# Two pools for the experts' first rooms, pinned first loads, and pools at multiples of 1 KB

## The chip, the core and the metric

The kernel runs on one core of a Trainium2 chip. The core has five engines with queues of their own: TensorE (PE in the profile; its weight loads are PEld), VectorE (DVE), ScalarE (ACT), GpSimd (POOL) and SyncE (SP). SP computes nothing here; it issues the loads of the weights to 16 DMA engines. The data lie in a memory of 128 partitions, in which the program places tiles from pools.

The metric is the device time of one execution in microseconds (us), as the median of several runs.

## The reference

Two blocks follow each other on 256 tokens of width 1024, all in float32. The first is a hybrid layer (attention and a gated delta rule). The second has a mixer with two groups of heads and then a layer of experts:

```python
def second_block(x, p, positions, w_in, ...):
    ...
    mixed = jnp.concatenate([rmsnorm_2(o_m, g_out_mla[i]), rmsnorm_2(o_s, g_out_sb[i])], axis=-1)
    h = h + mixed @ w_o[i]
    h = h + moe(rmsnorm_2(h, g_moe[i]), w_router[i], b_router[i], w_gu[i], b_gu[i], w_dn[i], b_dn[i])
    u = rmsnorm_2(h, g_ple[i])
    h = h + jax.nn.sigmoid(u @ w_ple_gate[i]) * (p[i] @ w_ple_proj[i])

def moe(u, w_router, b_router, w_gu, b_gu, w_dn, b_dn):
    """Top-4-of-32 clamped-SwiGLU experts on u (B, S, D)."""
    logits = jnp.dot(xt, w_router) + b_router
    top_logit, top_e = lax.top_k(logits, TOP_K)
    ...
        hh = jnp.dot(xs, w_gu[e]) + b_gu[e]
        glu, lin = jnp.split(hh, 2, axis=-1)
        act = glu * jax.nn.sigmoid(SWIGLU_ALPHA * glu) * (lin + 1.0)
        return jnp.dot(act, w_dn[e]) + b_dn[e]
```

There are 32 experts. `w_gu` of one is 1024 x 2048 and `w_dn` is 1024 x 1024, 12 MB together, and each is read once: 384 loads of 1 MB (1,048,576 bytes).

## The kernel before

**Stages.** The first block and the mixers of the second run up to about 557 us. There `w_in`, `w_uq`, `w_ukv` and `w_o` come in through three rooms `raw` of the pool `st` (8 KB of each partition, one load each), are split into a high and a low part (`piece`, `split`: ACT copies, DVE subtracts, lines 315 and 316), and PE multiplies. Then the router chooses, and the experts run from about 582 us on. In that stage the weights are not split: PE multiplies straight from the rooms that the loads fill (line 1370).

**The experts.** `units` puts the experts in pairs, but for one that stands alone with twice the rows and one single at the end. A pair takes 16 loads of `w_gu` (eight steps of one load for each of the two experts) and 8 of `w_dn`. `pieces` yields the loads in the order in which PE uses them, and `run` consumes them in that order.

**The rooms.** `load` takes its rooms in a fixed turn from the list `raws`. For the experts the list is: four rooms `raw` of the pool `raw2`, three rooms `raw` of `st`, two `whi` and two `wlo` of `raw2`, two `whi` and two `wlo` of `st`. These are 15 rooms of 8 KB. `ahead` (line 1148) asks for the first 11 loads and `refill` (line 1489) for all others. In SP's queue 15 loads stand ahead of the first one that has to wait for an expert's product, that of a room whose content PE has used. A room is loaded again once PE has used what is in it.

**What lies under the rooms.** The pool `raw2` is opened where the pools of the mixers have been closed. Those are `wa` (eight tiles `w4` of 4 KB, 32 KB in all: the name `soon` in the code) and above it `wb` (76 KB: the name `w`). `soon` has the latent vectors, the tokens' queries and keys, and in the end the scores of the second half of the latent attention, `mla(1)`: its last readers are the transposes in `softmax_T` (line 385; the helper's line 304 in the profile). `wb` has all else, up to the turning of the last heads' output (`out_T`, line 1030, and the split at its end). `raw2` has eight rooms, 64 KB: the first four lie over `wa`, the others over the foot of `wb`. The framework lets the first load into a pool wait until all that lay under that pool has been read.

**What sets the order.** Each engine runs its own queue in order, and a wait at its head holds back what stands behind it. A scheduler of the framework sorts the instructions within the queues, except those that the code pins with `tc.keep_in_program_order` (the products and transposes of the experts' stage). The loads are not pinned. SP's queue also holds every load to at most eight in flight, by eight semaphores in turn (`DMAHW0` to `DMAHW7`).

```python
    raw2 = ctx.enter_context(tc.tile_pool(name="raw2", bufs=1))

    raws[:] = [(raw2, "raw", RAW2), (st, "raw", RAW), (raw2, "whi", 2), (raw2, "wlo", 2), (st, "whi", HL), (st, "wlo", HL)]
    parts.append((raw2, 2))
    ...
            ready = ahead(order, RAW + RAW2 + 4)
```

Of the kernel before, what the change touches and what calls it, by code (L numbers as in the profile page):

```python
# [7 lines left out]
F32 = mybir.dt.float32  # L8
# [7 lines left out]
P = 128  # L16
# [51 lines left out]
def tile_net(ctx: ExitStack, tc: tile.TileContext, a: dict, dbg=None):  # L68
    nc = tc.nc
    V, A, G, T, SY = nc.vector, nc.scalar, nc.gpsimd, nc.tensor, nc.sync  # L70
    dbg = dbg or {}

    cst = ctx.enter_context(tc.tile_pool(name="cst", bufs=1))
    st = ctx.enter_context(tc.tile_pool(name="st", bufs=1))
    sm = ctx.enter_context(tc.tile_pool(name="sm", bufs=4))
# [17 lines left out]
    wr = cst.tile([P, 8, 32], F32, name="wr")  # L93
    bguT = cst.tile([P, 32, 16], F32, name="bguT")

    RAW, HL = 3, 2
    raws = [(st, "raw", RAW)]
    parts = [(st, HL)]
    count = [0, 0]

    def slots():
        return sum(n_ for _, _, n_ in raws)

    def load(src, kc, n, pool=None, rows="(k p) n -> p k n"):

        if pool is None:
            i = count[0] % slots()
            count[0] += 1
            for pool, name, nb in raws:
                if i < nb:  # L110
                    break
                i -= nb
        else:
            (pool, nb), name = pool, "raw"
        raw = pool.tile([P, 2048], F32, name=name, bufs=nb)
        SY.dma_start(raw[:, :kc * n].rearrange("p (k n) -> p k n", k=kc), src.rearrange(rows, p=P))
        return raw

    def piece(src, kc, n, raw=None, by=None):

        if raw is None:
            raw = load(src, kc, n)
        i = count[1] % sum(n_ for _, n_ in parts)
        count[1] += 1
        pool, nb = parts[0] if i < parts[0][1] else parts[1]
        hi = pool.tile([P, 2048], F32R, name="whi", bufs=nb)
        lo = pool.tile([P, 2048], F32R, name="wlo", bufs=nb)
        m = kc * n
        split(hi[:, :m], lo[:, :m], raw[:, :m], by)
        v = lambda t: t[:, :m].rearrange("p (k n) -> p k n", k=kc)  # L130
        return v(hi), v(lo)

    def rows_piece(W, i, pool=None):
        nh, k0 = i // 2, (i % 2) * 4
        return load(W[k0 * P:(k0 + 4) * P, nh * 512:(nh + 1) * 512], 4, 512, pool)
# [255 lines left out]
    def rope(wk, dst, src, cos2, sin2, nh):  # L391
# [5 lines left out]
        V.tensor_tensor(t2[:, :, 16:32], src[:, :, 0:16], bm(sin2[:, 16:32], nh), ALU.mult)  # L397
        V.tensor_tensor(dst, t1, t2, ALU.add)

    keep = Pool(ctx.enter_context(tc.tile_pool(name="keep", bufs=1)), w4=4)  # L400

    ORDER = "01kstvo"
# [2 lines left out]
    pp = cp.enter_context(tc.tile_pool(name="pp", bufs=4, space=bass.MemoryType.PSUM))  # L405
    with ExitStack() as c1:
        both = ctx.enter_context(tc.tile_pool(name="both", bufs=1))
        pm = c1.enter_context(tc.tile_pool(name="ps", bufs=4, space=bass.MemoryType.PSUM))
        c2 = c1.enter_context(ExitStack())
        wk = c2.enter_context(tc.tile_pool(name="wk", bufs=1))  # L410
# [12 lines left out]
        for i in (2, 1):  # L423
            SY.dma_start(ctab[i], a["const"][:, cuts[i]:cuts[i + 1]])
        uinc, ustr, lstr, ones = (cc(k) for k in ("uinc", "ustr", "lstr", "ones"))
        first = [load(w_in[k0 * P:(k0 + 4) * P, 4096:4608], 4, 512) for k0 in (0, 4)]
        rows = [("conv_w", 96), ("gdn_norm_w", 1), ("g_cq_2", 3), ("g_ckv_2", 2),
                ("g_out_mla_2", 4), ("g_out_sb_2", 4), ("g_attn_2", 8), ("g_ple_2", 8)]
        vr = wk.tile([P, P], F32, name="vrow1")
        at = 0  # L430
        for n, k in rows:
            voff[n] = 16 + at
            src = a[n]
            src = src.rearrange("o t (c p) -> (o t c) p", p=P) if n == "conv_w" else src.rearrange("o (c p) -> (o c) p", p=P)
# [679 lines left out]
    RAW2 = 4  # L1114

    raw2 = ctx.enter_context(tc.tile_pool(name="raw2", bufs=1))

    raws[:] = [(raw2, "raw", RAW2), (st, "raw", RAW), (raw2, "whi", 2), (raw2, "wlo", 2), (st, "whi", HL), (st, "wlo", HL)]
    parts.append((raw2, 2))
    NE = 32  # L1120
    NJ = 15
    wgu = a["w_gu_2"].rearrange("o e d f -> (o e d) f")
# [4 lines left out]
    def pieces(units):  # L1127


        for i in range(len(units) + 1):  # L1130
            if i < len(units):
                rs = [p["row"]() for p in units[i]["places"]]
                for k in range(8):
                    for r in rs:
                        yield wgu[bass.ds(r + k * P, P)], 1, 2 * D, "(k p) n -> p k n"
            if i:
                rs = [p["row"]() for p in units[i - 1]["places"]]
                for q in range(4):
                    for r in rs:
                        yield wdn[bass.ds(r + q * 2 * P, 2 * P)], 2, D, "(p k) n -> p k n"  # L1140
            if i == EMB:
                yield a["w_ple_proj_2"][0], 2, D, "(k p) n -> p k n"
# [4 lines left out]

    def ahead(order, n, pool=None):

        return [(load(src, kc, m, pool, rows), kc, m) for src, kc, m, rows in (next(order) for _ in range(n))]  # L1150

    def in_register(ap):

# [8 lines left out]
    with ExitStack() as c3:  # L1162
# [43 lines left out]
        with ExitStack() as c4:  # L1206
# [6 lines left out]
            for i in range(1, NE):  # L1213
                if len(units[-1]["places"]) == 1 and DBL not in (i, i - 1):
                    units[-1]["places"].append(places[i])
                else:
                    units.append(unit([places[i]], i))
            order = pieces(units)
            ready = ahead(order, RAW + RAW2 + 4)
            rr, ut = [], []  # L1220

# [262 lines left out]
        def run(units, order, ready, more=None, room=None):  # L1484
# [11 lines left out]
            def nxt():  # L1496
                if not ready:
                    ready.extend(ahead(order, 1))
                raw, kc, m = ready.pop(0)
                return raw[:, :kc * m].rearrange("p (k n) -> p k n", k=kc)  # L1500
# [279 lines left out]
```

## Time and profile before

| | |
|---|---|
| Time, median of 3 runs | 1570.43 us (1569.9 to 1571.59) |
| The profiled execution | 1570.8 us, its span 1568.9 us |
| PE busy | 1431.5 us, 91% of the span |
| DVE, ACT, POOL busy | 39%, 27%, 2% |
| Read from memory | 483.48 MB |

The span is the time from the first to the last recorded instruction; 1.9 us of the profiled execution's time lie around it. Busy shares are averages over stages that have different limits, so the view that matters is the one that cuts the span into stretches. A matmul's row shows its whole way through the array, and matmuls overlap, so a PE that is busy all the time can still have room. In a timeline a row starts with its start and its length in us; `x4` merges four instructions, and the bracket at the end says how long the engine was idle ahead of it and what ended that.

### The profile page before, as it was taken

To read this page: it belongs to the slowest core of one execution; us is meant where nothing else is said; L and a number is where in the kernel's file an instruction comes from. 1 tells how busy PE (TensorE), PEld (TensorE's weight loads), DVE (VectorE), ACT (ScalarE), POOL (GpSimd) and SP (SyncE) were. 2 spreads that over 40 slices of the span, in tenths; PEclk is the share of its full clock that TensorE was granted. 3 is DMA by queue.
4 is the path that set the end of the run, shared out by engine and by line. 5 is a ranking of instruction groups with operands and counts; after the bars stand their busy time and mean duration, and the time that the engine had idled before them with its cause. 6 is when DMAs were issued, how large, how long until landed. Compare 5 with 4: busy or idle time off the path is not lost. (4 is left out here: it accounts for less than half of the span.)

```text
span 1568.9 us, 20018 instructions
## 1 busy us (share of the span) xinstructions
PE 1431.5 (91%) x7922; PEld 883.2 (56%) x7922; DVE 619.3 (39%) x1215; ACT 418.6 (27%) x638; POOL 27.1 (2%) x39
## 2 busy tenths in 40 slices
PE   6999998999889989989888998999988889989887
PEld 6889898999689864424334334434433324424335
DVE  6868865456656662112123122112312202302236
ACT  5543644443447621101001001101100101101124
POOL 0000100000000000000000000000000000000000
PEclk9999999999899989999999999999999999999998
DMA  7544244355344189999999999999999999999981
GB/s 241 163 150 150 90 141 130 108 188 173 127 132 141 55 345 421 421 421 421 421 421 419 421 421 421 421 421 420 421 421 421 421 420 420 421 422 421 421 350 67
DMA packets 108541, 487.58 MB, mean 311 GB/s; under 512 B 14766, under 2 KB 23356, under 8 KB 59292
## 3 DMA queue, kind: packets, MB, share of 16 engines
q1 hardware_dynamic: 108300, 485.87, 78.2%
q8 instruction: 64, 1.05, 0.3%
q0 software_dynamic: 144, 0.39, 0.1%
q14 instruction: 33, 0.27, 0.0%
HBM read 483.48 MB, written 2.75 MB: 310 GB/s over the span
## 5 line engine op out<-in xcount | busy, mean ns | idle before, releaser
L1370 PE MATMUL ph<-raw,xs 128*64 128x512 f32 (+1 forms) x936 | 241.7, 594 | 5.7 <-DMA raw<-in_w_gu_dram 5.6
L1370 PE MATMUL ph<-wlo,xs 128*64 128x512 f32 (+1 forms) x552 | 192.3, 594 | 4.8 <-DMA wlo<-in_w_gu_dram 4.8
L1370 PE MATMUL ph<-whi,xs 128*64 128x512 f32 (+1 forms) x560 | 194.6, 594 | 2.0 <-DMA whi<-in_w_gu_dram 2.0
L316 DVE TENSOR_TENSOR wlo<-raw,whi 128x2048 fp32r<-128x2048 f32 (+4 forms) x73 | 158.0, 2165 | 91.8 <-ACT whi L315 91.7
L212 PE MATMUL pm<-w,wlo 128*128 128x256 f32 x640 | 182.5, 286 | 6.6 <-DVE wlo L316 6.6
L210 PE MATMUL pm<-w,whi 128*128 128x256 f32 x640 | 185.1, 290 | 3.3 <-ACT whi L315 3.3
L1557 DVE COPY hs<-ph 128x512 f32<-128x512 f32 x34 | 23.5, 692 | 406.4 <-PE ph L1370 406.4
L211 PE MATMUL pm<-w,whi 128*128 128x256 f32 x640 | 183.0, 286 | 0.0
L315 ACT CAST whi<-raw 128x2048 fp32r<-128x2048 f32 (+4 forms) x73 | 131.9, 1806 | 141.3 <-PE pm L211 88.1
L1370 PE MATMUL pm<-raw,act 128*64 128x512 f32 (+1 forms) x520 | 137.9, 597 | 29.0 <-DMA raw<-in_w_dn_dram 29.0
L1370 PEld LDWEIGHTS ph<-raw,xs 128*64 128x64 f32 (+1 forms) x936 | 78.1, 138 | 144.9 <-issue 130.8
L1557 ACT COPY hs<-ph 128x512 f32<-128x512 f32 x34 | 19.9, 586 | 412.6 <-PE ph L1370 412.6
L212 PEld LDWEIGHTS pm<-w,wlo 128*128 128x128 f32 x640 | 124.0, 194 | 7.5 <-DVE wlo L316 7.5
L210 PEld LDWEIGHTS pm<-w,whi 128*128 128x128 f32 x640 | 124.3, 194 | 4.1 <-ACT whi L315 3.9
L211 PEld LDWEIGHTS pm<-w,whi 128*128 128x128 f32 x640 | 124.5, 194 | 0.3
L1460 DVE SCALAR_TENSOR_TENSOR yl<-pm,gs,yh 128x512 fp32r<-128x512 f32 x32 | 24.0, 750 | 251.1 <-ACT yh L1459 250.4
L1370 PEld LDWEIGHTS ph<-wlo,xs 128*64 128x64 f32 (+1 forms) x552 | 61.6, 139 | 83.1 <-issue 72.8
L1370 PEld LDWEIGHTS ph<-whi,xs 128*64 128x64 f32 (+1 forms) x560 | 60.8, 138 | 81.5 <-issue 73.8
L1370 PEld LDWEIGHTS pm<-raw,act 128*64 128x64 f32 (+1 forms) x520 | 42.5, 137 | 113.6 <-issue 62.3
L1370 PE MATMUL pm<-wlo,act 128*64 128x512 f32 (+1 forms) x256 | 87.8, 597 | 11.8 <-DMA wlo<-in_w_dn_dram 11.5
L1459 ACT ACTIVATE yh<-pm,gs 128x512 fp32r<-128x512 f32 x32 | 22.0, 687 | 266.6 <-PE pm L1370 265.1
L1370 PE MATMUL pm<-whi,act 128*64 128x512 f32 (+1 forms) x248 | 82.5, 597 | 10.4 <-DMA whi<-in_w_dn_dram 10.4
(399 smaller groups left out, 1921.4 us busy)
## 6 DMA issues: line engine op xcount, KB each, us to landing
raw<-in_w_gu_dram SPq DMA_DIRECT2D x117, 1024.0 KB, 19.8
whi<-in_w_gu_dram SPq DMA_DIRECT2D x70, 1024.0 KB, 19.8
wlo<-in_w_gu_dram SPq DMA_DIRECT2D x69, 1024.0 KB, 19.8
raw<-in_w_dn_dram SPq DMA_DIRECT2D x65, 1024.0 KB, 19.8
raw<-in_w_in_dram SPq DMA_DIRECT2D x46, 1024.0 KB, 5.6
wlo<-in_w_dn_dram SPq DMA_DIRECT2D x32, 1024.0 KB, 20.0
whi<-in_w_dn_dram SPq DMA_DIRECT2D x31, 1024.0 KB, 19.8
raw<-in_w_branch_a_dram SPq DMA_DIRECT2D x4, 1024.0 KB
```

The lines of the kernel that those rows point to most:

```text
L210: T.matmul(o, hi[:, k, ns], xh[:, k0 + k], start=first, stop=False)
L211: T.matmul(o, hi[:, k, ns], xl[:, k0 + k], start=False, stop=False)
L212: T.matmul(o, lo[:, k, ns], xh[:, k0 + k], start=False, stop=last)
L315: A.copy(hi, src)
L316: (by or V).tensor_tensor(lo, src, hi.bitcast(F32), ALU.subtract)
L1370: return tc.keep_in_program_order(T.matmul(*x_, **y_))
L1459: A.activation(yh[:, ns], yp[n_], AF.Copy, scale=b["gs"])
L1460: V.scalar_tensor_tensor(yl[:, ns], yp[n_], b["gs"], yh[:, ns].bitcast(F32), ALU.mult, ALU.subtract)
L1557: (V.tensor_copy if j // 2 else A.copy)(b["hs"][j // 2][:, j % 2 * 512:j % 2 * 512 + 512], hp[j])
```

## The change

Three things are done, and none changes what is computed.

- The pool `raw2` keeps the four rooms `raw`. The two `whi` and two `wlo` move to a new pool `raw3`, opened right behind it. `raw2` is then 32 KB, as large as `wa` was, and `raw3` lies over the foot of `wb`.
- `load` gets a flag `pin`, and `ahead` sets it: the loads that `ahead` issues stand in SP's queue in the order of the program.
- Three tiles that nothing reads or writes (`gap0` of 640 bytes of each partition in `cst`, `gap1` of 320 in `sm`, `gap2` of 192 in `both`) move the pools behind them. The first room of `st` starts at byte 22,912 of the partition before and at 23,552 (23 x 1024) after; the first of `raw2` at 104,320 before and at 105,472 (103 x 1024) after. Before, every room starts 128 bytes behind a multiple of 256.

```diff
+    cst.tile([P, 160], F32, name="gap0")
...
-    def load(src, kc, n, pool=None, rows="(k p) n -> p k n"):
+    def load(src, kc, n, pool=None, rows="(k p) n -> p k n", pin=False):
...
-        SY.dma_start(raw[:, :kc * n].rearrange("p (k n) -> p k n", k=kc), src.rearrange(rows, p=P))
+        d_ = SY.dma_start(raw[:, :kc * n].rearrange("p (k n) -> p k n", k=kc), src.rearrange(rows, p=P))
+        if pin:
+            tc.keep_in_program_order(d_)
...
+    sm.tile([P, 80], F32, name="gap1", bufs=1)
...
+        both.tile([P, 48], F32, name="gap2")
...
-
-    raws[:] = [(raw2, "raw", RAW2), (st, "raw", RAW), (raw2, "whi", 2), (raw2, "wlo", 2), (st, "whi", HL), (st, "wlo", HL)]
-    parts.append((raw2, 2))
+    raw3 = ctx.enter_context(tc.tile_pool(name="raw3", bufs=1))
+
+    raws[:] = [(raw2, "raw", RAW2), (st, "raw", RAW), (raw3, "whi", 2), (raw3, "wlo", 2), (st, "whi", HL), (st, "wlo", HL)]
+    parts.append((raw3, 2))
...
-        return [(load(src, kc, m, pool, rows), kc, m) for src, kc, m, rows in (next(order) for _ in range(n))]
+        return [(load(src, kc, m, pool, rows, True), kc, m) for src, kc, m, rows in (next(order) for _ in range(n))]
```

The queues of PE, DVE, ACT and POOL hold the same instructions in the same order as before. Only SP's queue changes, at one place, and the semaphores that eight of PE's products wait for. In SP's queue, behind the last load of `w_o`, this stood before (raw_5386 to raw_5392 are the four rooms of `raw2`, raw_5394 to raw_5398 those of `st`):

```order
L116 DMA raw_5137<-in_w_o_2_dram 128x4x512 [waits DMAHW0_49,DVE_49]
L116 DMA raw_5394<-in_w_gu_2_dram 128x2048 [waits DMAHW1_49,DVE_49]
L116 DMA raw_5396<-in_w_gu_2_dram 128x2048 [waits DMAHW2_49,DVE_49]
L116 DMA raw_5398<-in_w_gu_2_dram 128x2048 [waits DMAHW3_49,DVE_49]
L116 DMA raw_5386<-in_w_gu_2_dram 128x2048 [waits DVE_49,PE_49]
L116 DMA raw_5388<-in_w_gu_2_dram 128x2048
L116 DMA raw_5390<-in_w_gu_2_dram 128x2048
L116 DMA raw_5392<-in_w_gu_2_dram 128x2048
L116 DMA whi_5400<-in_w_gu_2_dram 128x2048
L116 DMA whi_5402<-in_w_gu_2_dram 128x2048 [waits DMAHW4_49]
```

And now, in the same place (raw_5392 to raw_5398 are the rooms of `raw2`, raw_5400 to raw_5404 those of `st`, whi_5406 the first of `raw3`):

```order
L117 DMA raw_5140<-in_w_o_2_dram 128x4x512 [waits DMAHW0_49,DVE_49]
L117 DMA raw_5392<-in_w_gu_2_dram 128x2048 [waits PE_49]
L117 DMA raw_5394<-in_w_gu_2_dram 128x2048
L117 DMA raw_5396<-in_w_gu_2_dram 128x2048
L117 DMA raw_5398<-in_w_gu_2_dram 128x2048
L117 DMA raw_5400<-in_w_gu_2_dram 128x2048 [waits DMAHW1_49,DVE_49]
L117 DMA raw_5402<-in_w_gu_2_dram 128x2048 [waits DMAHW2_49,DVE_49]
L117 DMA raw_5404<-in_w_gu_2_dram 128x2048 [waits DMAHW3_49,DVE_49]
L117 DMA whi_5406<-in_w_gu_2_dram 128x2048 [waits DVE_49,PE_49]
L117 DMA whi_5408<-in_w_gu_2_dram 128x2048 [waits DMAHW4_49]
```

The four loads of `raw2` have moved from behind the three of `st` to ahead of them, and the wait on DVE and PE for `wb` has moved from them to the first load of `raw3`. What they wait for themselves now is one instruction of PE, the last of the transposes of `mla(1)`.

On PE the first products of the first pair of experts waited for their loads so before:

```order
L1370 MATMUL ph_5683<-raw_5386,xs_5586 64x512 [waits DMAHW7_49,Activation_49]
L1370 MATMUL ph_5683<-raw_5388,xs_5586 64x512 [waits DMAHW0_49]
...
L1370 MATMUL ph_5683<-raw_5390,xs_5586 64x512 [waits DMAHW1_49]
L1370 MATMUL ph_5683<-raw_5392,xs_5586 64x512 [waits DMAHW2_49]
...
L1370 MATMUL ph_5683<-raw_5394,xs_5586 64x512 [waits DMAHW4_49]
```

And now:

```order
L1376 MATMUL ph_5689<-raw_5392,xs_5592 64x512 [waits DMAHW4_49,Activation_49]
L1376 MATMUL ph_5689<-raw_5394,xs_5592 64x512 [waits DMAHW5_49]
...
L1376 MATMUL ph_5689<-raw_5396,xs_5592 64x512 [waits DMAHW6_49]
L1376 MATMUL ph_5689<-raw_5398,xs_5592 64x512 [waits DMAHW7_49]
...
L1376 MATMUL ph_5689<-raw_5400,xs_5592 64x512 [waits DMAHW0_49]
```

The products stand where they stood; each waits for the semaphore that its load now has.

## Rows read from the trace of the kernel before

**Rows 1.** Page: DMA busy tenths and GB/s in 40 slices of 39.2 us.

```profile
DMA  7544244355344189999999999999999999999981
GB/s 241 163 150 150 90 141 130 108 188 173 127 132 141 55 345 421 421 421 421 421 421 419 421 421 421 421 421 420 421 421 421 421 420 420 421 422 421 421 350 67
```

**Rows 2.** Busy time by stretch: us, PE, PEld, DVE, ACT, POOL, PEclk, DMA share, GB/s.

```profile
520.00:531.00 11.00, 10.06 (x68) 8.45 (x67) 9.32 (x15) 6.70 (x9) 0.00 (x0) 1.00 0.00 0
...
537.00:549.00 12.00, 11.85 (x49) 9.59 (x50) 5.70 (x8) 4.39 (x8) 0.75 (x2) 0.86 0.00 1
...
960.00:1060.00 100.00, 97.81 (x400) 45.00 (x400) 25.03 (x56) 12.01 (x20) 0.00 (x0) 1.00 1.01 421
```

**Rows 3.** Timeline of SP's queue, 509 to 600 us: start, length, what, count.

```profile
531.13 27.90 SPq L116 DMA_DIRECT2D raw<-in_w_gu_dram  x7
559.08 0.98 SPq L116 DMA_DIRECT2D whi<-in_w_gu_dram  x2
560.12 1.46 SPq L116 DMA_DIRECT2D wlo<-in_w_gu_dram  x2
563.77 4.61 SPq L116 DMA_DIRECT2D whi<-in_w_gu_dram  x2
570.18 2.94 SPq L116 DMA_DIRECT2D wlo<-in_w_gu_dram  x2
585.51 10.63 SPq L116 DMA_DIRECT2D raw<-in_w_gu_dram  x7
```

**Rows 4.** Timelines of SP's queue in short stretches (549, 556 and 587 us).

```profile
549.24 0.34 SPq L116 DMA_DIRECT2D raw<-in_w_gu_dram  x1
...
556.41 2.63 SPq L116 DMA_DIRECT2D raw<-in_w_gu_dram  x5
...
587.63 0.36 SPq L116 DMA_DIRECT2D raw<-in_w_gu_dram  x1
```

**Rows 5.** Timeline of PE: the transposes, and the first products of the experts.

```profile
521.35 0.66 PE L304 MATMUL pm<-C,w 128*128 128x128 f32 x4 [0.94 <-ACT w L386]
...
551.24 0.63 PE L304 MATMUL pm<-C,w 128*128 128x128 f32 x4 [0.57 <-DVE w L1038]
...
575.16 6.74 PE L1370 MATMUL pm<-dd,w 128*128 128x128 f32 x32 [1.11 <-DVE dd L1383]
581.83 10.94 PE L1370 MATMUL ph<-raw,xs 128*64 128x512 f32 x49
```

**Rows 6.** Stretches of 1 us about two issues, columns as in rows 2.

```profile
550.00:551.00 1.00, 0.67 (x3) 0.20 (x2) 0.39 (x1) 0.00 (x0) 0.55 (x1) 1.00 0.70 131
...
557.00:558.00 1.00, 1.00 (x6) 0.81 (x5) 0.96 (x2) 0.33 (x1) 0.00 (x0) 1.00 0.61 82
```

**Rows 7.** DMA of 557 to 592 us: queue, packets, MB, share of 16 engines.

```profile
q1 hardware_dynamic: 1890, 13.81, 97.7%
```

**Rows 8.** PE's waits for DMA, 592 to 760 us: us in total, times, longest.

```profile
PE pm L1370 <- DMA wlo<-in_w_dn_dram: 2.6, 2, 1.3
PE pm L1370 <- DMA raw<-in_w_dn_dram: 2.6, 2, 1.3
PE ph L1370 <- DMA raw<-in_w_gu_dram: 1.8, 2, 1.3
PE ph L1370 <- DMA wlo<-in_w_gu_dram: 1.3, 1, 1.3
PE pm L1370 <- DMA whi<-in_w_dn_dram: 1.3, 1, 1.3
```

**Rows 9.** PE's waits for DMA, 1460 to 1540 us, and its last expert products.

```profile
PE pm L1370 <- DMA raw<-in_w_dn_dram: 3.9, 3, 1.3
...
1521.64 1.94 PE L1370 MATMUL pm<-wlo,act 128*64 128x512 f32 x8 [0.28 <-SPq L1623]
```

**Rows 10.** DMA of 403 to 405 us, then of 590 to 1500 us, as rows 7.

```profile
q1 hardware_dynamic: 662, 0.76, 106.8%
...
q1 hardware_dynamic: 52602, 382.16, 101.0%
```

## The prediction

> **What bounds the kernel now.** I read the 40 slices first: from the 16th on DMA is at 9 tenths or more and moves 421 GB/s, until the tail [rows 1]. So the experts' stage is set by the stream of weights: 1,048,576 bytes at 421 GB/s are 2.49 us a load. PE is nearly as busy there (97.81 of 100 us in one stretch), but in no slice does the rate of the stream fall for it [rows 1, 2]. PE waits for loads early in the stage, 2.6 + 2.6 + 1.8 + 1.3 + 1.3 = 9.6 us by 760 us [rows 8], and again in the last unit, where its last products come at 1521.64 us [rows 9]. A stage of this kind ends earlier only if the stream starts earlier, has fewer bytes, or runs faster.
>
> Then I looked at where the stream starts. The slice ahead of it is half empty [rows 1], and closer up DMA does nothing at all from 520 to 531 us and from 537 to 549 us [rows 2]. SP's queue tells why. The load at 531.13 us is the first of the weights of the experts, into a room of `st`; the second follows at 549.24 and the third at 556.41 us, and five go out from there: this third one and the four of `raw2` [rows 3, 4]. The four could not go earlier for two reasons. They stood behind the three of `st`, and their own wait was for the last readers of `wb`, of which PE's transposes at 551.24 us are one [rows 5].
>
> From 556.41 us on everything comes at once: 5 raw, 4 whi and 4 wlo, 13 loads [rows 3, 4]. Queue 1 moves 13.81 MB between 557 and 592 us [rows 7]. 13 loads are 13.63 MB; the other 0.18 MB are 0.4 us of the next load. So that next load, the 16th of the stage, begins to flow at 592 - 0.4 = 591.6 us. SP had issued it at 585.51 us [rows 3], when PE was through with the first room: PE's products start at 581.83 us, behind the gather that starts at 575.16 us and waits for VectorE, not for a load [rows 5]. From 591.6 us on the stream never stops. The 6 us between the issue and the flow are the place where an earlier start pays.
>
> **The pools in two, and the order.** These two go together. The four loads of `raw2` now stand first, and wait only for the last transposes of `mla(1)`. Those are the four at 521.35 us, the third of three such groups, released by ACT's copy as the queue says; they take 0.66 us [rows 5]. So the four are issued at about 522.0 us, into a DMA that is empty until 531 us [rows 2]. An issue takes 0.34 us in SP [rows 4]. From issue to flow it is 1.0 us: the load of 549.24 us flows from about 550.3 us (70% of the stretch to 551), the one of 556.41 us from about 557.4 us (61% of the stretch to 558) [rows 4, 6]. Four loads then take 4 x 2.49 = 10 us, to 533 us. The load of 531.13 us queues behind them for some 2 us, is through by 536 us, and nobody asks for it before 582 us. Cost of the early transfer: I put it at nothing, for DMA is idle there, and no other load stands in SP's queue between that of `w_o` and 531.13 us. If it did slow the mixers, the bound is that of the stretch that it lies in: PE is busy 10.06 of 11 us there [rows 2], and 5% on it would be 0.5 us.
>
> The waits on the later loads stay. The second and third of `st` go out when their rooms are split, at 549.24 and 556.41 us as before, and `raw3` takes the wait for `wb` that `raw2` had, right behind. From 556.41 us on there are 13 - 4 = 9 loads. They are through four loads earlier, 591.6 - 10.0 = 581.6 us. Then all 15 rooms are full, and DMA has nothing to do until PE frees the first: the 16th load is issued at 585.51 us as before and flows from 586.5 us. The lead of the stream is 591.6 - 586.5 = **5.1 us**. So of the 10 us moved into the gap about half is given back in a new gap from 581.6 to 586.5 us.
>
> Does the stream run on from there? The 17th load was issued at 587.63 us before [rows 4], with 1.0 us more 588.6 us, and the 16th occupies DMA until 589.0 us. After that PE frees two rooms per step, and a step is 8 products: 49 products with starts from 581.83 us on cover 10.94 us [rows 5], so at about 3.4 us a step and 1.7 us a load rooms come free faster than 2.49 us. Nothing is late next. If the lone 16th load starts slowly, as the one in the stretch to 551 us does (131 GB/s in it) [rows 6], up to 0.6 us of the lead are lost: 4.5 us. Upward, 0.1 us of issue to flow is all that I see: 5.2 us.
>
> Does the lead reach the end? PE takes it only when it next waits for a load. With 9.6 us of such waits by 760 us [rows 8] the 5.1 us are used up before that point, and from there on all is as before, 5.1 us earlier, down to the last load, for which PE waits too [rows 9]. The tail behind it does not change.
>
> **The gaps.** Three tiles that nobody uses cost no instruction. They shift every address behind them by 640, 960 or 1,152 bytes. I take nothing for that; the two rivals on it are below.
>
> **Sum.** The span of 1568.9 us less 5.1 is 1563.8 us, and with the 1.9 us around it 1565.7 us; the profiled execution was 0.4 us over the median of 1570.43 us, so the median comes to **1565.3 us**, 0.32% less.
>
> **The rivals.** *PE is the bound after all, and the lead is lost.* For it: PE is busy 97.81 of 100 us from 960 to 1060 us [rows 2]. Against it: the 9.6 us of waits ahead of that [rows 8]. It would give 1570.4 us. Chance 8%.
>
> *The order alone, without the shorter wait.* If the loads of `raw2` still waited for the readers of `wb`, that is to 551.9 us, and stood first, the loads of 531.13 and 549.24 us would wait behind them: 15 loads from 552.9 us, at 2.49 us and with the 1.8 us that the 13 lost before (591.6 - 557.4 - 13 x 2.49), end at 592.1 us. That is no change, 1570.9 us. Against it stands the queue, which names one wait on PE and none on DVE. Chance 4%.
>
> *The new addresses make the stream faster.* Each room starts 128 bytes behind a multiple of 256 before and on one now. If a piece of 8,192 bytes paid for those 128 bytes too, it would get 1.6% shorter, and 930 us of stream (591.6 to 1521.64) would give 14.5 us; PE has 2.2% of room where it is busiest [rows 2], so most of it would come through, with the lead some 17 to 19 us: 1552 us. The loads of 288 columns of `w_in_2` (1,152 bytes a piece, at 403 to 405 us) speak weakly against it: 1,152 is 4.5 times 256, so every second piece in a room starts on a multiple, and 662 of them take 106.8% x 16 x 2 us / 662 = 51.6 ns in the mean, while the large ones take about 315 (101.0% x 16 x 910 us / some 46,700 of the 52,602, the others being the small ones that signal) [rows 10]; a slope between the two sizes leaves 8.6 ns fixed for each, no sign of a cheap half, though a mean can't exclude it. [...] Chance 6%.
>
> *The new addresses make it slower.* The same 1.6% with the other sign, from rooms that now all start at the same place within 1 KB: 14.5 - 5.1 = 9.4 us more, 1580 us. It decides from 5.1 / 930 = 0.55% on, that is where the stream falls from 421 to under 418.7 GB/s. Nothing in the rows moves the rate by that much [rows 1]; nothing excludes it either, since all rooms lie alike before. Chance 5%.
>
> **How the numbers follow.** The forecast has 77%. Its own range is 4.0 to 5.5 us of gain and some 0.8 us of spread as in the runs before: 1564 to 1567 us. The range of 8 in 10 takes in lost parts of the lead and small effects of the addresses: 1561 to 1569 us. A measurement of this kernel can tell 0.2%, 3.1 us, from no change. Faster by more: 75 + 6 = 81%. Within: 2 + 8 + 4 = 14%. Slower: 5%.
>
> **What would show it.** In the profile after: four loads issued at about 522 us and DMA full from 523 to 533 us; DMA idle from about 581.6 to 586.5 us; PE's first products at 581.8 us as before; 421 GB/s from 592 us on; fewer waits of PE for loads before 760 us, by about 5 us, and the last products at about 1516.5 us. I am wrong if the four loads go out only after 549 us, if the gap at 582 us is missing or longer than 6 us, or if the rate of the stream is not 421 GB/s.

## The result and the profile after

The changed kernel takes 1549.05 us (median, 1547.85 to 1555.33) beside 1570.74 us of the kernel before, a ratio of 0.9866 (0.9852 to 0.988): 1.34% less, 21.7 us. The forecast was 1565.3 us, and its range ended at 1561. A second comparison, last below, gave 0.9879 (0.9857 to 0.9902). The profiled execution took 1555.33 us, its span 1553.5 us; it was the longest of its four.

The page of the kernel after, DMA busy tenths and GB/s in 40 slices of 38.8 us, as [rows 1]:

```profile
DMA  7444343355425468999999999999999999999981
GB/s 246 163 149 132 104 150 108 114 184 185 144 86 189 163 273 363 426 427 427 426 427 426 426 427 427 426 427 427 426 427 426 427 427 426 426 428 426 426 354 65
```

Where the kernel before moves 421 GB/s, this one moves 426 to 428, from the first full slice to the last. That is what the forecast did not have. The stretches of [rows 2], and the new gap (us, PE, PEld, DVE, ACT, POOL, PEclk, DMA share, GB/s):

```profile
520.00:531.00 11.00, 10.02 (x64) 8.30 (x63) 9.32 (x19) 8.20 (x10) 0.00 (x0) 1.00 0.49 191
...
537.00:549.00 12.00, 10.35 (x54) 8.39 (x54) 5.25 (x10) 5.68 (x10) 1.10 (x2) 1.00 0.12 48
...
583.00:588.00 5.00, 5.00 (x26) 1.78 (x26) 3.61 (x24) 0.59 (x1) 0.00 (x0) 1.00 0.07 15
...
960.00:1060.00 100.00, 98.61 (x401) 45.50 (x402) 23.00 (x53) 11.52 (x19) 0.00 (x0) 1.00 1.01 427
```

The stretch from 520 us on, empty before, now has loads; the gap that the forecast expected behind the first 15 loads is there, within 583 to 588 us. SP's queue, as [rows 3, 4] (in the first row the x7 of a coarse view are the four loads of `raw2` and the three of `st`; the last three rows show parts of it closer up):

```profile
524.38 33.54 SPq L117 DMA_DIRECT2D raw<-in_w_gu_dram  x7
558.25 0.80 SPq L117 DMA_DIRECT2D whi<-in_w_gu_dram  x2
...
586.75 10.63 SPq L117 DMA_DIRECT2D raw<-in_w_gu_dram  x7
...
524.38 2.00 SPq L117 DMA_DIRECT2D raw<-in_w_gu_dram  x4
...
550.44 0.33 SPq L117 DMA_DIRECT2D raw<-in_w_gu_dram  x1
...
557.60 0.33 SPq L117 DMA_DIRECT2D raw<-in_w_gu_dram  x1
```

PE's rows that answer to [rows 5, 9]: the transposes that the four loads wait for, the first products of the experts, the last ones:

```profile
523.70 0.66 PE L307 MATMUL pm<-C,w 128*128 128x128 f32 x4 [0.98 <-ACT w L389]
...
583.07 10.94 PE L1376 MATMUL ph<-raw,xs 128*64 128x512 f32 x49
...
1504.54 1.89 PE L1376 MATMUL pm<-wlo,act 128*64 128x512 f32 x8
```

And PE's waits for DMA from 592 to 760 us, as [rows 8]; they sum to 5.9 us, 9.6 before:

```profile
PE pm L1376 <- DMA raw<-in_w_dn_dram: 3.8, 3, 1.3
...
PE pm L1376 <- DMA wlo<-in_w_dn_dram: 1.2, 1, 1.2
PE ph L1376 <- DMA raw<-in_w_gu_dram: 0.9, 1, 0.9
```

The measure that I use from here on is the **experts' stretch**, from the start of the first products to the start of the last eight: 1521.64 - 581.83 = 939.8 us before [rows 5, 9], 1504.54 - 583.07 = 921.5 us after. It lost 18.3 us. It leaves out the mixers ahead and the tail behind, which vary between executions (last experiment).

### The profile page after: what moved, and what is told of

The parts are those of the page before. It is cut to its first block, busy times and chain, and to the rows that moved or that the text cites. A ratio compares the mean times of both kernels' runs of the same rounds, so it can differ in the third digit from the quotient of the medians.

```text
span 1553.5 us, 20018 instructions
## 1 busy us (share of the span) xinstructions
PE 1433.5 (92%) x7922; PEld 887.9 (57%) x7922; DVE 619.3 (40%) x1215; ACT 419.0 (27%) x638; POOL 27.1 (2%) x39
```

## The experiments

**The two halves apart.** `gaps_only` is the kernel before with the three unused tiles and nothing else; `no_gaps` is the changed kernel without them, so new pools and pinned loads at the old addresses.

```diff
+    cst.tile([P, 160], F32, name="gap0")
+    sm.tile([P, 80], F32, name="gap1", bufs=1)
+        both.tile([P, 48], F32, name="gap2")
```

> The kernel before with the three unused tiles alone. Theory R (the addresses set the rate of the stream): 427 GB/s in the experts' stage instead of 421, over 368 loads at 2.46 instead of 2.49 us about 12 us, so some 1558.5 us; no lead, DMA full from 557 us on. Rival S (the two pools and the pinned order bring nearly all, the gaps nothing): 421 GB/s and 1570.5 us.

> The changed kernel without the three unused tiles: two pools and pinned loads at the old addresses. Theory R: the lead alone, four loads at about 522 us, DMA empty from about 581.6 to 586.5 us, 421 GB/s afterwards, 1565.5 us (5 us less than before). Rival S: 427 GB/s and about 1549 us.

Measured: `gaps_only` 1558.67 us, ratio 0.9917 (0.99 to 0.9933); `no_gaps` 1564.78 us, ratio 0.996 (0.9947 to 0.9972). The stretch from 600 to 700 us, of `gaps_only`:

```profile
600.00:700.00 100.00, 95.90 (x478) 39.67 (x474) 22.52 (x52) 13.44 (x21) 0.00 (x0) 1.00 1.01 427
```

and of `no_gaps`, with its last products:

```profile
600.00:700.00 100.00, 97.74 (x492) 40.91 (x488) 22.51 (x52) 13.45 (x21) 0.00 (x0) 1.00 1.01 421
...
1516.86 1.94 PE L1373 MATMUL pm<-wlo,act 128*64 128x512 f32 x8 [0.30 <-SPq L1626]
```

The first products of both, and the last ones of `gaps_only`:

```profile
582.39 10.09 PE L1373 MATMUL ph<-raw,xs 128*64 128x512 f32 x46
...
1509.81 1.89 PE L1373 MATMUL pm<-wlo,act 128*64 128x512 f32 x8
...
582.14 10.09 PE L1373 MATMUL ph<-raw,xs 128*64 128x512 f32 x46
```

The rate goes with the gaps alone, the lead with the order alone. The experts' stretch is 927.4 us with the gaps (12.4 less than before) and 934.7 us with the order (5.1 less, the lead as forecast). Together that is 17.5 of the 18.3 us. The other 0.8 us is about what kernels alike in order and rate differ by (`no_gaps` 934.7, `off128` 934.5 and `off64` 935.2 us; `gaps_only` 927.4 and `others_off` 926.8 us), so I don't assign it.

**Which multiple.** The changed kernel, with 256, 128 or 64 bytes more in the first gap, moves every room by that much.

```diff
-    cst.tile([P, 160], F32, name="gap0")
+    cst.tile([P, 224], F32, name="gap0")
```

(192 for `off128`, 176 for `off64`.)

> The changed kernel with 256 bytes more ahead of the rooms: every room starts on a multiple of 256 but on none of 512 or 1024. [...] If it has to be 1 KB or 512: 421 GB/s and 1561 to 1565 us.

> The changed kernel with 128 bytes more ahead of the rooms: every room 128 bytes behind a multiple of 1 KB. Theory R: the slow rate, 421 GB/s, as without gaps: 1561 to 1565.5 us. If the old rooms were slow for where in 1 KB they lay (384 and 896) and not for being off 256: 427 GB/s and 1549 us.

> The changed kernel with 64 bytes more in its first gap: the rooms lie 64 bytes behind a multiple of 256 (and all rooms alike). Theory R (any place off a multiple of 256 is slow): 421 GB/s and 1565 us, as with 128. If 64 is as good as 256: 427 GB/s and 1549 to 1550 us.

Measured: `off256` 1550.09 us, ratio 0.9865 (0.9848 to 0.9881), 427 GB/s; `off128` 1564.82 us, 0.9955 (0.9938 to 0.9972), 421 GB/s; `off64` 1565.96 us, 0.9957 (0.9943 to 0.9971), 421 GB/s. The stretches from 600 to 700 us, in this order:

```profile
600.00:700.00 100.00, 97.70 (x494) 40.29 (x491) 22.52 (x52) 13.44 (x21) 0.00 (x0) 1.00 1.01 427
...
600.00:700.00 100.00, 97.83 (x494) 41.19 (x492) 22.52 (x52) 13.45 (x21) 0.00 (x0) 1.00 1.01 421
...
600.00:700.00 100.00, 97.47 (x492) 40.20 (x489) 22.52 (x52) 13.45 (x21) 0.00 (x0) 1.00 1.01 421
```

So multiples of 256 bytes do, and neither 512 bytes nor 1 KB is needed; 64 and 128 bytes off cost the same.

**Whose address: the rooms or the rest.** Both kernels are `gaps_only` with 128-byte tiles ahead of or behind the rooms. In `rooms_off` the 15 rooms go back to 128 bytes behind a multiple of 256, and the tiles behind `sm` move by multiples of 256 bytes only; in `others_off` the rooms stay on such multiples, and those tiles move 128 bytes off.

```diff
     st = ctx.enter_context(tc.tile_pool(name="st", bufs=1))
+    st.tile([P, 32], F32, name="lead_st", bufs=1)
...
-    sm.tile([P, 80], F32, name="gap1", bufs=1)
+    sm.tile([P, 112], F32, name="gap1", bufs=1)
...
     raw2 = ctx.enter_context(tc.tile_pool(name="raw2", bufs=1))
+    raw2.tile([P, 32], F32, name="lead_raw2", bufs=1)
...
         kp = c3.enter_context(tc.tile_pool(name="kp", bufs=1))
+        kp.tile([P, 32], F32, name="lead_kp", bufs=1)
```

(`others_off` is the same without the tile in `st`.)

> The kernel before with the three gaps, and with two unused tiles of 128 bytes ahead of the rooms (in st and in raw2) and two of 128 bytes behind them (in sm and kp): the 15 rooms lie 128 bytes behind a multiple of 256 again, all other tiles lie as with the gaps alone, to 256 bytes. Theory R (it is where the loads land): the stream falls back to 421 GB/s, and the time to 1570.5 us (1568.5 to 1572). Rival O (it is where the other tiles lie, that PE reads beside the rooms and DVE and ACT write): the stream stays at 427 GB/s and the time at 1558.7 us.

> The other half: the kernel before with the three gaps and 128 bytes more behind st's rooms (in sm), ahead of raw2's first room and behind its last (in kp): the 15 rooms lie on multiples of 256, all tiles behind st and outside raw2 lie 128 bytes elsewhere, as in the kernel before. Theory R (where the loads land): 427 GB/s and 1558.7 us (1557 to 1560.5). Rival O (the other tiles): 421 GB/s and 1570.5 us.

Measured: `rooms_off` 1568.19 us, ratio 0.9985 (0.9974 to 0.9996); `others_off` 1557.13 us, 0.9908 (0.988 to 0.9937). The stretch from 600 to 700 us, of `rooms_off`:

```profile
600.00:700.00 100.00, 93.66 (x468) 38.88 (x464) 22.50 (x52) 13.45 (x21) 0.00 (x0) 1.00 1.01 421
```

and of `others_off`:

```profile
600.00:700.00 100.00, 95.50 (x478) 39.75 (x476) 22.51 (x52) 13.45 (x21) 0.00 (x0) 1.00 1.01 427
```

What counts is where the loads land. The other tiles, moved 128 bytes off, left the rate as it was. (Tiles of `sm` itself move with the rooms of `st`; they do so in `st_off` below too, and there the stream keeps 426 GB/s.) `rooms_off` lies a little below its range; its experts' stretch is 940.7 us, no shorter than before, so what it gained lies outside that stretch (last experiment).

**Does PE's reading slow the writes?** `few_products` is the kernel before with many products of the experts left out (for pairs, every column block but the first is multiplied only in the first and the last of the eight chunks). That is half of a pair's products, not two thirds as the expectation says. All loads stay.

```diff
                     sl = slice(j * 512, j * 512 + 512)
+                    if kd == "pair" and j and 0 < chunk < nchunks - 1:
+                        continue
```

> The kernel before, its addresses too, without most products of the experts: of the pairs, a column block other than the first is multiplied only with the first and the last of the eight chunks (about two thirds of the products are left out). Every load is still issued, and every room still has a reader. Theory R (the place of the rooms alone sets the pace): PE is busy less than half of the stage, the stream stays at 421 GB/s, and as the stream sets the end the time is 1570 us (1567 to 1572). Rival X (PE reading from the rooms holds the writes back): 426 to 427 GB/s and 1555 to 1560 us.

Measured: 1573.47 us, ratio 1.0016 (1.0005 to 1.0028), 1.5 us above the theory's range. The stretch from 592 to 1480 us, of the kernel before and of this one:

```profile
592.00:1480.00 888.00, 808.29 (x3804) 339.38 (x3801) 190.83 (x420) 98.95 (x159) 0.75 (x1) 1.00 1.01 421
...
592.00:1480.00 888.00, 687.62 (x2384) 251.29 (x2385) 189.61 (x418) 98.67 (x159) 0.74 (x1) 0.88 1.01 421
```

All of PE's matmuls are counted here; of the experts' own the trace has 1632 rows instead of 3072, and the stream stays at 421 GB/s. PE's busy time falls less than expected, to 77% of the stretch, partly at a lower granted clock (0.88 in the mean, 1.00 in the kernel before). PE now waits 184 us for loads from 592 to 1500 us instead of 63, and still the experts' stretch (941.1 us) does not fall: in the kernel before the stream sets the end, not PE. The run halves the reads and does not remove them, so by itself it can't tell whether some reading is needed. The trace of `no_gaps` can: from 572 to 574 us 64% of the stream's packets already take longer than 310 ns (most take 309 in an undisturbed stream, below), and the first product that reads what this stream has loaded comes at 582.14 us. PE's reads are not the cause.

**A price for each load, or a state of the stream?** All these have the three gaps. In `st_off` 7 rooms are off the multiple (those of `st`: `lead_st` and the larger `gap1` of the diff above), in `raw2_off` the 8 of `raw2` (`lead_raw2` and `lead_kp`), in `eleven_off` 11 that follow each other in the turn (`lead_st`, the larger `gap1`, `lead_raw2`, and 128 bytes ahead of the first `whi` of `raw2`).

> The kernel before with the three gaps, but the 7 of the 15 rooms that lie in st are 128 bytes behind a multiple of 256, the 8 of raw2 on one. Theory P (each misplaced load pays for itself): loads into st take 2.485 us, those into raw2 2.453 us, in the mean 7 x 421 and 8 x 427 make 424 GB/s, and the time is 1558.7 + 7/15 x 12 = 1564.3 us. Rival S (a misplaced load upsets the pace of those that follow): loads into raw2 are slow too, 421 GB/s and 1570 us.

> The mirror of st_off: the kernel before with the three gaps, but the 8 rooms of raw2 lie 128 bytes behind a multiple of 256 and the 7 of st on one; in the turn of the rooms 4 loads off, 3 on, 4 off, 4 on. Theory S2 (a state of the stream: while loads land off the multiple, packets get stretched more and more; loads on it bring the 16 engines back to 309 ns): the runs of 4 are too short for it, 426 to 427 GB/s and 1556 to 1559 us. Rival Z (only the place of raw2's rooms counts, since those of st showed no effect): 421 GB/s and 1568 to 1571 us.

> The same with 11 of the 15 rooms off the multiple, one behind the other in the turn (the four of st's whi and wlo, the four raw of raw2, the three raw of st), and only the whi and wlo of raw2 on it. Theory S2: in a run of 11 loads (27 us) the share of stretched packets climbs from nothing towards the 0.74 that it has with all rooms off, and the four loads on the multiple bring it back; in the mean 424 to 426 GB/s and 1560 to 1564 us. If four loads on the multiple are not enough to bring it back: 421 GB/s and 1568 us. If the place of raw2's whi and wlo alone counts: 427 GB/s and 1557 us, with no climb within the run.

Measured: `st_off` 1556.06 us, ratio 0.9902 (0.9873 to 0.993); `raw2_off` 1560.52 us, 0.993 (0.9883 to 0.9977); `eleven_off` 1565.51 us, 0.9948 (0.9921 to 0.9974). Worked out from the traces: the mean rate of 592 to 1480 us, the experts' stretch, and the share of the 8-KB packets between 592 and 1490 us that took over 310 ns (a packet is the piece of a load that one DMA engine moves into one partition; with all rooms on the multiple nearly all take 309 ns):

```
              rooms off    run off    GB/s   stretch us   packets over 310 ns
gaps_only       0 of 15       0        427      927.4           0.2%
st_off          7 of 15       4        426      929.0           2.8%
raw2_off        8 of 15       4        426      930.4           9.3%
eleven_off     11 of 15      11        424      934.8          36.7%
rooms_off      15 of 15      all       421      940.7          73.8%
```

A price for each load would put `st_off` at 7/15 of the 13.3 us between the first and the last line, 6.2 us; it costs 1.6. (Its time is even below that of `gaps_only`; the stretch is not, so that difference too lies outside.) Both theories of `st_off`'s expectation fell. What the runs bear out is the state that `raw2_off`'s expectation put in their place: packets are stretched more and more while loads land off the multiple, and loads on it end that. One turn of the rooms in `eleven_off`, the end of a run off the multiple, the four loads on it, and the first eight of the next run off it:

```profile
630.00:647.50 17.50, 17.50 (x83) 6.18 (x81) 1.38 (x2) 1.17 (x2) 0.00 (x0) 1.00 1.01 421
647.50:657.30 9.80, 7.90 (x36) 2.97 (x33) 0.00 (x0) 0.00 (x0) 0.00 (x0) 1.00 1.01 428
657.30:667.20 9.90, 9.38 (x64) 6.84 (x60) 4.74 (x13) 3.18 (x5) 0.00 (x0) 1.00 1.01 426
667.20:677.10 9.90, 9.32 (x41) 3.40 (x43) 6.39 (x15) 1.89 (x3) 0.00 (x0) 1.00 1.01 420
```

Four loads off the multiple still run at 426 GB/s, the next four at 420. Worked out from the packets' records, the share of those over 310 ns by the load's place in the turn, in the mean over the stage:

```
four loads on the multiple    0.18 0.02 0.00 0.00
eleven loads off it           0.01 0.03 0.07 0.39 0.70 0.71 0.70 0.73 0.74 0.70 0.47
```

(The packets are cut into loads as their records come, and engines that are late or early blur the borders: hence 0.47 at the end and 0.18 at the start; another way to cut them moves single numbers by up to 0.1.) The share grows manyfold within four loads and saturates with the fifth, earlier than the climb over the whole run that I expected; so `eleven_off` lies a little above its 1560 to 1564 us, at the rate expected, 424 GB/s. `raw2_off` too lies 1.5 us above what was expected: its runs of four reach 0.25 and 0.44 in their last load. That of `st_off` reaches 0.17, so the length of the run alone does not set the share; why these differ is open. Nor does the share alone tell the rate: in `off64` 91% of the packets take over 310 ns and most often 312, in the kernel before 73%, and both have the mean of 314.0 ns and 421 GB/s.

**The changed kernel once more,** for a second profile, as nothing so far explains the last 3 us between 18.3 and 21.7.

> The changed kernel as it is, for a second profile and a narrower interval: its first profile was its longest execution, 1555.33 us beside 1547.85 to 1549.43. From the first product of the experts to their last ones the traces gave 939.8 us before, 934.7 without the gaps, 927.4 with the gaps alone and 921.5 with both. Theory: that stretch is 921.5 us again and the median 1549 us; the 3 us that the median gained beyond those 18.3 us lie ahead of the first product, which then comes at about 579 us (583.07 in the first profile). Rival: they lie behind the last products: the first product at 582 to 583 us, and a tail 3 us shorter than the 47.3 us of the kernel before.

Measured: 1550.62 us (1547.72 to 1553.94) beside 1571.38 us; the profiled execution was the shortest, 1547.72 us, span 1545.9 us. Its first and last products:

```profile
577.13 10.94 PE L1376 MATMUL ph<-raw,xs 128*64 128x512 f32 x49
...
1498.52 1.89 PE L1376 MATMUL pm<-wlo,act 128*64 128x512 f32 x8
```

The experts' stretch is 921.4 us, the same to 0.1 us. The tail is 47.4 us (47.3 before, 49.0 in the first profile of after), and the first product comes at 577.13 us instead of 583.07, so the theory holds for the place. But the two profiles are of one program, and differ by 5.9 us ahead of the first product: the records of PE's granted clock hold 37.5 us at the lower of the two levels in them (0.5 and 1.0) there in the first, 20.5 us in the second (34.1 us in the kernel before, whose first product comes at 581.83 us). So the part ahead of the experts varies between executions by more than the 3 us in question. The other kernels say the same: the median less the experts' stretch is 630.9 us before and 627.5 in the first runs of after, and over all kernels here it lies between 627.1 (`st_off`) and 632.4 us (`few_products`), with 627.5 for `rooms_off`, whose rooms lie off the multiple, and 631.3 for `gaps_only`, whose rooms lie on it. I take the 3 us for that variation, and the place of the rooms does not go with it; that other new addresses help the mixers isn't excluded.

## Why the prediction was wrong

- **The lead: right.** The four loads go out 0.68 us behind the transposes (524.38 - 523.70), forecast 0.65. The early transfer costs nothing that shows: PE is busy 10.02 of the 11 us from 520 us on, 10.06 before. The gap is there; from the trace the 15th load ends at 583.8 us, 2.2 us later than forecast, and the 16th flows at 587.75 us, 1.0 us behind its issue and 1.2 us later than forecast, as the first product was. The gain is 5.1 us in the experts' stretch, measured alone in `no_gaps`; its last products come at 1516.86 us, forecast 1516.5. That it meets the forecast to 0.1 us is luck: `off128` and `off64`, with the same order, gain 5.3 and 4.6 us.
- **Where PE takes the lead up: right, but not by the sign that was named.** From 592 to 760 us PE waits 7.8 us for loads in `no_gaps`, only 1.8 less than before, where about 5 was forecast; a window cut in time holds more work when the work comes earlier. Compared product by product, counted from the first, `no_gaps` is 4.3 us ahead where the kernel before stands at 748 us and 4.9 us at 778 us, and it ends 5.1 us ahead. (The prediction calls 49 rows 49 products; each product leaves two rows, and its 3.4 us for a step of 8 products are right for 16 rows.)
- **The gaps: the step that failed.** "I take nothing for that" is the term that was mis-sized: it is 12.4 us in `gaps_only`, more than twice the lead. Behind it stood the rate of the stream, which the sum held at 421 GB/s to the end; with the rooms on multiples of 256 bytes it is 427.
- **The rival that named it** had 6% and was priced at 17 to 19 us with the lead; the experts' stretch lost 18.3. Its size was right, its mechanism not, so the agreement is partly luck. It supposed that a piece off the multiple takes longer by itself. Before and after, a packet most often takes 309 ns, and hardly one takes less; the slow stream is one in which most of them take a few ns more (mean 314.0 ns before, 309.5 after), and that state needs several loads to arise. No run shows the term that its sum took, 128 bytes paid for on each piece of 8,192 (1.6%); it was the author's supposition. By an estimate from the same sum, a piece 64 bytes off would pay half of that, 64 / 8,192 = 0.8%. The runs show 421 GB/s for both, and `st_off` shows 426 GB/s with 7 of 15 rooms off the multiple, beside 427 with none.
- **The evidence that I weighed could not tell.** The pieces of 1,152 bytes [rows 10] are a burst of 2 us, and this state takes several loads of 2.45 us to build up. The row that would have told stood in the trace of before, and I did not use it. It is the first part of the same stage, with the same rooms:

```profile
561.00:570.00 9.00, 8.54 (x60) 7.46 (x58) 4.31 (x15) 5.67 (x12) 1.10 (x2) 1.00 1.02 427
```

  The stream of before starts at 427 GB/s and falls to 421 afterwards. Its packets say it more sharply than a rate over 9 us: from 561 to 573 us at most 5 in 100 take over 310 ns, from 573 to 576 us 35, and in the stage some 73. I took 421 for what the DMA engines can do, because every slice of the stage reads alike [rows 1]; it was what they did in that state.
- **PE as the bound: excluded.** With 427 GB/s PE is busy 98.61 of 100 us in its fullest stretch (its rows overlap: in the kernel before a row `ph<-raw,xs` takes 594 ns in the mean, and 49 of them cover 10.94 us [rows 5]), and still it follows the stream: its waits for loads from 592 to 1500 us sum to 47.6 us after and 63.3 before. The 15.7 us between them are near the 18.3 us that the stretch lost; 592 to 1500 us cuts each trace at other places.
- **The new addresses make it slower:** it had 5%, and the sign was the other one; that all rooms start at the same place within 1 KB costs nothing that shows. Before, those of `st` and of `raw2` start at two places, 384 and 896 bytes behind a multiple of 1 KB; `no_gaps` has these two and `off128` a single one, both off 256, and their stretches are 934.7 and 934.5 us.

What stays open is why a stream off the multiple falls out of step, and what starts it. (The records name no DMA engine; packets are put together to one engine by each starting where another ends.) In the trace of before, a fetch of instructions at 563.9 us holds up one DMA engine (one packet of 855 ns at 564.76 us). The packets behind it on that engine take 318, 309, 315, 309, 319 ns, while those of the other 15 stay at 309 from 564 to 571 us; at 571.8 us a second fetch holds up another engine, and from 573 us on others lengthen too. In `gaps_only` the first fetch (one packet of 855 ns at 566.96 us) leaves all that follow it there at 309 ns until 573 us. But no fetch is needed: `no_gaps`, which pauses before its 16th load, is back at 309 ns for some 12 us after the pause (share of longer packets at most 0.1 from 588 to 600 us) and then slows (0.7 at 606 us), with no fetch in its records between 587 and 614 us. So aligned loads or a pause end the state, as these runs show; what starts it, and how it passes from one engine to the others, they do not.

## What to carry over

Let the rooms that a saturated stream of loads fills start on multiples of 256 bytes of the partition (tried here with pieces of 8 KB: 427 GB/s instead of 421); look at the addresses of the pools, since a small tile ahead moves everything behind it. Before you call a rate the limit of the DMA engines, look for the fastest stretch of the same loads in the same trace and ask why it isn't held. And judge a move of work into an idle gap by the gap that it leaves behind: here 10 us moved gained 5.1.

## What the hardware showed that was not expected

- Loads of 1 MB in pieces of 8,192 bytes run at 427 GB/s (2.453 us a load in the median) into rooms on multiples of 256 bytes and at 421 GB/s (2.486 to 2.487 us) 64 or 128 bytes behind one: 1.4%.
- The loss is not paid by each piece. In `eleven_off` the share of packets over 310 ns saturates with the fifth load in a row (0.70) and two aligned ones undo it (0.18, then 0.02); with 8 of 15 rooms misplaced in runs of four it costs 3.0 of 13.3 us (`raw2_off`).
- PE's reads of the same rooms did not matter here: 421 GB/s with 1632 rows of the experts' products as with 3072, and the slow state is there before PE reads any of them (64% of the packets over 310 ns from 572 to 574 us in `no_gaps`, first product at 582.14 us).
